# A hybrid attention and mLSTM block: the mLSTM output stored as two float32r parts and reloaded by DMA alone, one head earlier

## The chip, the core and the metric

The kernel runs on one core of a Trainium2 chip. The core has five engines that work side by side, each through a queue of its own, in order: TensorE (PE, matmuls; its weight loads are shown apart as PEld), VectorE (DVE), ScalarE (ACT), GpSimd (POOL) and SyncE (SP), which here does nothing but issue DMA transfers. Sixteen DMA engines move the data. The metric is the time of one execution on the device in microseconds; the median of several runs counts.

## The reference

One decoder layer on 1,024 tokens of width 1,024. A projection feeds two mixers side by side, differential attention (8 heads) and an mLSTM (4 heads of width 256, chunkwise); both outputs are projected, gated and added. A squared-ReLU MLP follows.

```
h = rms_norm(x, norm_mix_g) * (1 + sc_a) + sh_a
aq, ak, av, mq, mk, mv, mo, mi, mf, ga, gm = split(h @ w_in)
...
ya = diff_attention(aq[0], aq[1], ak[0], ak[1], av, lam, bias_by_dist)      # 8 heads, causal softmax
...
hm = mlstm_chunkwise(mq, mk, mv, mi + b_igate, mf + b_fgate)                # 4 heads
hm = rms_norm(hm, mhn_g)
ym = sigmoid(mo) * hm
merged = sigmoid(ga) * (ya @ w_a) + sigmoid(gm) * (ym @ w_m)
x = x + gt_a * (merged @ w_out)
h = rms_norm(x, norm_ffn_g) * (1 + sc_f) + sh_f
x = x + gt_f * (square(relu(h @ w_ff1)) @ w_ff2)
```

The change concerns `ym`, between the mLSTM that makes it and `ym @ w_m` that uses it.

## The kernel before

**Numbers in two parts.** Every float32 operand of a large matmul is used as a high part (rounded to float32r by an ACT copy) and a low part (DVE: source minus high part); `mm3` then issues three matmuls: high by high, high by low, low by high. `split_lo` (line 139) is the DVE half of such a split, wherever it stands.

**Stages.** After the projections come the four mLSTM heads (about 490 to 745 us in the trace), then the eight attention heads (about 745 to 1,214 us), then the products with `w_a`, `w_out` and the MLP.

**mLSTM, `ml_core`.** A head has four groups g of 256 tokens. The string in the code gives the order of its steps: P (load `ex`, the decay factors), K (`keys`: transpose the keys, scale, split; line 987), W (`weights`: scores `st`, times `ex` at line 958, split into `sw` at 960 and 961), S and C (matmuls `num`, `cps`), I, N (normalise), F (`finish`). `finish(g)` multiplies `hs` by the norm and by `hd["o"][g]` (the gate `mo`; line 1052), transposes four blocks into one PSUM bank `tp` (1058), copies them out with the factor `mhg` on ACT (1063) and stores 256 KB into `ym_d` in DRAM (1064). The last group's F is carried over into the next head.

**Attention, `at_core`.** For a head, S (`soft`: logits `lg` at line 1220, bias and running minimum on DVE at 1226, exp on ACT at 1230, combination on DVE at 1239), T (`turn_p`: transposes 1253, ACT `pth` 1256, DVE `ptl` 1257), Y (`sums`: matmuls `pv`, 1273) and F, for eight blocks of 128 queries. The dots in its string are places where `weave` puts steps of a list `filler`, spread evenly. In heads 0 to 6 the filler is the q/k projection of the next head (`at_qk`, matmuls `ps<-w,hT`, 192 of them for a head) and its preparation (`at_prep`: `raw`, `qe`, `kb`; `qe` is completed by a copy DMA `qe<-qe`, line 1196). In head 7 the filler is the reload of `ym` and 24 steps of `ym @ w_m` (`m_unit`, 12 matmuls `ps<-ym,w` in a step, two steps to a part). The rest of the 32 steps runs after head 7. A part also loads a gate `sg` (1316), applies tanh (1317), multiplies on DVE (1320), which frees its PSUM bank, and stores to `mb_d`.

**Reload.** `reload` has eight steps: a 512 KB DMA from `ym_d` into `w_st` (1305), two ACT copies into the high parts of `ym` (1308), two DVE subtractions into the low parts (line 139). `ym` takes over the four 2 MB tiles (`tag="x"`) that held the layer input `hT`: tile 0 of it (tokens 0 to 511) is free when the first half of head 7's q/k projection is done, tile 1 (tokens 512 to 1,023) when all of it is.

**What sets the order.** The order in each queue is fixed when the kernel is built: a scheduler takes the steps in the order in which the code gives them and moves instructions ahead where their operands allow it. Tiles rotate within a tag; `f` has 5 buffers (among them `ex`, `hs`/`it`, `sg`, `pth`, `ptl`), `m` has 4 (`mo`, `yt`), `w_st` has 2, and PSUM has 8 banks: `mm` 2 (parts of `m_unit` among them), `pa` 3, `pb` 3. DMAs that SP issues use eight semaphores in turn, so a DMA also waits until the one eight places ahead of it has landed.

Of the kernel before, what the change touches and what calls it, by code (L numbers as in the profile page):

```python
# [8 lines left out]
F32 = mybir.dt.float32  # L9
F32R = mybir.dt.float32r  # L10
BF16 = mybir.dt.bfloat16
AF = mybir.ActivationFunctionType
ALU = mybir.AluOpType
# [4 lines left out]
P = 128  # L18
S = 1024
D = 1024  # L20
NT = S // P
KT = D // P
AH = 8
# [13 lines left out]
def kernel(  # L37
# [7 lines left out]
    nc = tc.nc  # L45
# [4 lines left out]
    dp = ctx.enter_context(tc.tile_pool(name="dp", bufs=1, space=DRAM))  # L50
    wp = ctx.enter_context(tc.tile_pool(name="wp", bufs=2))
# [7 lines left out]
    def wt(tag, shape, name, dt=F32):  # L59
        return sp.tile(shape, dt, name=name, tag=tag, bufs=BUFS[tag])  # L60

    def bank(tag, name):
        return pp.tile([P, 512], F32, name=name, tag=tag, bufs={"mm": 2, "pa": 3, "pb": 3}[tag])


    ya_d = dp.tile([D, S], F32, name="ya_d")
    ym_d = dp.tile([D, S], F32, name="ym_d")
    sga_d = dp.tile([D, S], F32, name="sga_d")
    sgm_d = dp.tile([D, S], F32, name="sgm_d")
    mb_d = dp.tile([D, S], F32, name="mb_d")  # L70
# [39 lines left out]
    def row(v):  # L110
        return v.rearrange("o (k p) -> (o k) p", p=P)
# [22 lines left out]
    def split_lo(dst, src, hi, pool=None):  # L134

        if pool is None:
            turn[0] += 1
            pool = turn[0] % 2
        return (nc.gpsimd if pool else nc.vector).tensor_tensor(dst, src, hi.bitcast(F32), op=ALU.subtract)  # L139
# [136 lines left out]
    def run(steps):  # L276
        for f in steps:
            f()

    def weave(main, filler):  # L280

        n, done = main.count(None), 0
        for f in main:
            if f is not None:
                f()
            if f is None or not n:
                done += 1
                run(filler[(done - 1) * len(filler) // (n or len(main)):done * len(filler) // (n or len(main))])
# [56 lines left out]
    class Group:  # L345
# [35 lines left out]
        pool = (None, True,)[1:]  # L381
# [369 lines left out]
    def gate_unit(i):  # L751

        dst = (sga_d, sgm_d)[i // 4]
        f = (i % 4) * 256
        get_w = once(next_w)

        def out(ps, t, t0):
            sg = wt("f", [P, 512], "sg")
            nc.scalar.copy(sg, ps)
            nc.sync.dma_start(dst[f + t * P:f + (t + 1) * P, t0:t0 + 512], sg)  # L760

        return sum((
            feat_steps(hT, get_w, t * P, t0, "mm", lambda ps, t=t, t0=t0: out(ps, t, t0))
            for t in range(2) for t0 in (0, 512)
        ), [])
# [4 lines left out]
    class Conv(Group):  # L770
# [7 lines left out]
        pool = (False,)  # L778
# [34 lines left out]
    class Gate(Group):  # L813
# [7 lines left out]
        pool = (False,)  # L821
# [12 lines left out]
    class Tok(Group):  # L834
# [7 lines left out]
        pool = (False,)  # L842
# [82 lines left out]
    def ml_core(h, hd, more):  # L925
# [123 lines left out]
        def finish(g):  # L1049
            hs, ssh = state.pop(("hs", g))  # L1050
            for tt in range(2):
                nc.vector.scalar_tensor_tensor(
                    hs[:, tt, :], hs[:, tt, :], ssh[:, tt:tt + 1], hd["o"][g][:, tt, :], op0=ALU.mult, op1=ALU.mult
                )
            tp = bank("pa", "tp")
            for k in range(2):
                for tt in range(2):
                    nc.tensor.transpose(
                        tp[:, k * 256 + tt * P:k * 256 + (tt + 1) * P], hs[:, tt, k * P:(k + 1) * P], ident
                    )  # L1060
            yo = hs
            for k in range(2):
                nc.scalar.activation(yo[:, k, :], tp[:, k * 256:(k + 1) * 256], AF.Copy, scale=mhg[:, k:k + 1])
            nc.sync.dma_start(
                ym_d[h * 256:(h + 1) * 256, g * 256:(g + 1) * 256].rearrange("(k p) t -> p k t", p=P), yo
            )

        def step(f, g):
            return lambda: f(g)
# [3 lines left out]
        for w in ("P0 K0 P1 K1 W0 W1 P2 C0 S0 N0 W2 S1 I1 C1 F0 K2 I2 P3 N1 C2 S2 F1 W3 X0 X1 N2 I3 S3 X2 N3 F2" if h < MH - 1 else "P0 K0 P1 K1 W0 W1 C0 P2 S0 N0 W2 S1 I1 C1 F0 K2 I2 P3 N1 C2 S2 F1 W3 N2 I3 S3 N3 F2").split():  # L1073
            if w == ".":
                steps.append(None)
            elif w[0] == "X":
                if more:
                    i = int(w[1])
                    steps.append((lambda: more[0](0), lambda: more[1](0), lambda: more[1](1))[i])
            else:  # L1080
                steps.append(step(fs[w[0]], int(w[1])))
        return steps, [step(finish, 3)]


# [28 lines left out]
    def at_qk(h, hd):  # L1113

        get_w = once(next_w)
        hd["raw"] = {}

        def out(ps, hf, jj):
            if jj == 0:
                hd["raw"][hf] = wt("u", [P, 4, 256], "raw")  # L1120
            nc.scalar.copy(hd["raw"][hf][:, jj * 2:jj * 2 + 2, :], ps.rearrange("p (t c) -> p t c", t=2))

        return sum((
            tok_steps(hT, get_w, hf * 4 + jj * 2, "mm", lambda ps, hf=hf, jj=jj: out(ps, hf, jj))
            for hf in range(2) for jj in range(2)
        ), [])
# [170 lines left out]
        return steps, [lambda: finish(1)]  # L1297


    def reload(a, src, pool=None):  # L1300


        def step(t0, k):
            st = wp.tile([P, 2, 512], F32, name="w_st", tag="ws", bufs=2)
            nc.sync.dma_start(st, src[k * P:(k + 2) * P, t0:t0 + 512].rearrange("(k p) t -> p k t", p=P))
            for i in range(2):
                ah, al = a.at(k + i, t0, 512)
                nc.scalar.activation(ah, st[:, i, :], AF.Copy)
                split_lo(al, st[:, i, :], ah, pool)

        return [lambda t0=t0, k=k: step(t0, k) for t0 in (0, 512) for k in range(0, KT, 2)]

    def gated(src, f0, t0):

# [10 lines left out]
    def m_unit(ym, u):  # L1325

        get_w = once(next_w)

        def part(t, t0):
            f0 = u * 256 + t * P  # L1330
            box = []
            steps = feat_steps(
                ym, get_w, t * P, t0, "mm",
                lambda ps: nc.gpsimd.dma_start(mb_d[f0:f0 + P, t0:t0 + 512], box[0](ps)),
            )

            def start():
                box.append(gated(sgm_d, f0, t0))
                steps[0]()

            return [start] + steps[1:]

        return sum((part(t, t0) for t0 in (0, 512) for t in range(2)), [])
# [30 lines left out]
    for j in range(NT + 3):  # L1374
# [10 lines left out]
        if j == 2:  # L1385
# [4 lines left out]
            mhg = par.add(row(mhn_g), 2)  # L1390
# [99 lines left out]
    units = sum((gate_unit(i) for i in range(1)), [])  # L1490
# [10 lines left out]
    for h in range(MH):  # L1501
# [5 lines left out]
        filler = late + gate_unit(h + 1)  # L1507
# [9 lines left out]
    for h in range(AH):  # L1517
        core, nlate = at_core(h, heads[h], vts)
        filler = list(late)
        if h + 1 < AH:  # L1520
            filler += at_qk(h + 1, heads[h + 1])
            if h in AT_GATES:
                filler += gate_unit(AT_GATES[h])
            qs, ps = iter(filler), at_prep(h + 1, heads[h + 1])
            filler = [ps[int(w)] if w in "012345" else next(qs, lambda: None) for w in "qqqqqqqqq012345"] + list(qs)
        else:
            ym = ActX("ym")
            units = sum((m_unit(ym, u) for u in range(4)), [])
            gta = wt("b", [P, D], "gta")
            nc.sync.dma_start(gta, gt_d[0])  # L1530

            nc.vector.tensor_scalar(gta, gta, 0.5, None, op0=ALU.mult)
            wos = {}

            def fetch_wo(r):
                wos[r] = wt("u", [P, D], "wor")
                nc.sync.dma_start(wos[r], w_out[0][r * P:(r + 1) * P, :])

            def gate_wo(r):
                w = wos.pop(r)  # L1540
                nc.vector.tensor_tensor(w, w, gta, op=ALU.mult)
                nc.sync.dma_start(wo_d[r * P:(r + 1) * P, :], w)

            for r in range(8):
                units[12 + 2 * r] = lambda r=r, f=units[12 + 2 * r]: (fetch_wo(r), f())
                units[15 + 2 * r] = lambda r=r, f=units[15 + 2 * r]: (gate_wo(r), f())
            filler += reload(ym, ym_d, False) + units[0:12 * 2]
        weave(core, filler)
        late = nlate
        if h % 2 and h + 1 < AH:  # L1550
            vts = []
            run(at_v(h + 1, vts))
# [279 lines left out]
    class Ff1(Group):  # L1832
# [9 lines left out]
        pool = (False,)  # L1842
# [148 lines left out]
    def b_tile(i, tag, n):  # L1991
        if tag == "x":
            t = xp.tile([P, 2, 4, 512], F32R, name=f"b{n}", tag="x")
            B[i] = lambda k: (t[:, 0, k, :], t[:, 1, k, :])
        else:
            ts = [wt(tag, [P, 2, 512], f"b{n}", F32R) for _ in range(4)]
            B[i] = lambda k: (ts[k][:, 0, :], ts[k][:, 1, :])
# [46 lines left out]
    def left(g, order, load=False):  # L2044
        if load:
            g.load()
        g.weights(order)

    todo = dict(
        a=g0.p1, b=g1.p1, c=g2.load_first, d=g0.p2, e=g3.load_first, f=g1.p2, g=g2.p1, h=g2.p2, i=g3.p1, j=g3.p2,  # L2050
        k=lambda: left(g0, (7, 5), True), l=lambda: left(g1, (7, 5), True), m=g0.p7, n=g1.p7,
        t=lambda: b_tile(5, "x", "t1"),
# [118 lines left out]
    for n in range(7 * NC):  # L2171
# [7 lines left out]
        if n in whole:  # L2179
            q, t0, c0 = whole[n]  # L2180
            nc.sync.dma_start(q, xn_d[t0:t0 + 512, c0:c0 + 512].rearrange("(t p) c -> p t c", p=P))
        if n - 1 in rows:
            q, t0, c0, j = joins[n - 8]
            add(q[:, j], q[:, j], rows.pop(n - 1), False)
        if 7 <= n < 15:
            q, t0, c0, j = joins[n - 7]
# [54 lines left out]
```

## Time and profile before

| | us |
|---|---|
| runs: median (lowest to highest) | 2036.21 (2036.16 to 2036.49) |
| the profiled execution: time of the run, span of the trace | 2033.65, 2031.9 |
| PE busy over the span | 1970.7 (97%) |
| DVE busy | 1636.7 (81%) |
| ACT busy | 1053.0 (52%) |
| mLSTM, 540 to 748 us: PE busy, DVE busy | 200.47 and 132.00 of 208 |
| heads 5 to 7, 1,040 to 1,110 us: PE, DVE | 69.82 and 53.27 of 70 |
| head 7, 1,110 to 1,140 us: PE, DVE | 22.86 and 26.76 of 30 |

The span is that of the trace; the run's own time is 1.75 us longer. An engine's idle time is put down in the trace to whatever event ended it ("releaser"). A line number can be that of a helper: line 139 is every low part, so its rows are told apart by the tile they write (`ym`, `w_lo`). Matmul rows overlap (each is pipelined into the next), so the distance between two starts, not the listed duration, is what a matmul costs in a row of them.

### The profile page before, as it was taken

What the parts mean: (1) busy time and instruction counts of PE and PEld (TensorE: products, weight loads), DVE (VectorE), ACT (ScalarE), POOL (GpSimd) and SP (SyncE); (2) the same over time, 40 slices, a digit from 0 to 9 for tenths busy, and PEclk for the clock granted to TensorE, in tenths of its full rate; (3) what the DMA queues carried; (4) which work ended last, traced back from release to release, by engine and by line L of the source; (5) the groups of instructions that cost most, each with busy time, mean ns of one, the idle gap of its engine ahead of it and who ended that gap; (6) DMA issues with size and microseconds to landing.
All of it is one profiled execution on the core that took longest, in us unless ns stands there. A gap on an engine that the chain in (4) does not pass through costs nothing.

```text
span 2031.9 us, 30206 instructions
## 1 busy us (share of the span) xinstructions
PE 1970.7 (97%) x11193; PEld 1709.9 (84%) x11193; DVE 1636.7 (81%) x2883; ACT 1053.0 (52%) x1983; POOL 55.8 (3%) x150
## 2 busy tenths in 40 slices
PE   5999999999999999999999889999999999999999
PEld 5999998888888899999999668877788888888887
DVE  7977668988766568999978757999867668999896
ACT  5523224544566557777766534546645545433332
POOL 0000000000011000000000100000000000000000
PEclk7999999999999999999999999999999999999999
DMA  8376633335665442322223875603446446755531
GB/s 285 107 221 205 203 113 119 104 104 181 194 169 170 121 116 63 84 63 84 63 83 87 288 263 186 202 22 127 147 145 218 165 151 227 276 181 156 165 114 73
DMA packets 205386, 307.21 MB, mean 151 GB/s; under 512 B 14435, under 2 KB 115454, under 8 KB 205238
## 3 DMA queue, kind: packets, MB, share of 16 engines
q1 hardware_dynamic: 202358, 295.84, 45.9%
q0 software_dynamic: 2880, 9.44, 1.2%
q8 instruction: 88, 1.44, 0.3%
q14 instruction: 60, 0.49, 0.1%
HBM read 212.19 MB, written 84.64 MB: 146 GB/s over the span
## 4 chain that ended last, share of the span: by engine, by line
PE 77%; DVE 8%; DMA 6%; issue 4%; ACT 4%; POOL 1%; SPq 0%; DVEq 0%; POOLq 0%; ACTq 0%
PE cps L329 18%; PE pa L329 10%; PE pc L329 10%; PE pb L329 10%; PE pd L329 5%; PE ps L167 4%; PE ps L166 4%; PE ps L168 4%; PE lg L1220 3%; PE pv L1273 2%; DMA ex<-ea_d 1%; PE ops L586 1%; PE tp L1253 1%; DMA w<-in_w_ff_dram 1%; DMA xt<-in_x_dram 1%
## 5 line engine op out<-in xcount | busy, mean ns | idle before, releaser
L329 PE MATMUL cps<-t_op,s_op 128*128 128x512 f32 x2016 | 466.8, 393 | 2.1 <-DVE t_op L139 1.8
L329 PEld LDWEIGHTS cps<-t_op,s_op 128*128 128x128 f32 x2016 | 377.9, 188 | 88.1 <-DVE t_op L139 2.1
L321 ACT ACTIVATE w_op<-w_st 128x512 fp32r<-128x512 f32 (+1 forms) x197 | 135.9, 705 | 196.2 <-PE pb L329 60.0
L139 DVE TENSOR_TENSOR w_op<-w_st,w_op 128x512 fp32r<-128x512 f32 (+1 forms) x197 | 150.0, 780 | 27.2 <-ACT w_op L321 25.3
L166 PE MATMUL ps<-w_hi,hT 128*128 128x256 f32 x512 | 146.5, 286 | 0.0
L167 PE MATMUL ps<-w_lo,hT 128*128 128x256 f32 x512 | 145.9, 285 | 0.0
L168 PE MATMUL ps<-w_hi,hT 128*128 128x256 f32 x512 | 145.6, 284 | 0.0
L321 ACT ACTIVATE s_op<-act 128x1024 fp32r<-128x1024 f32 x56 | 59.0, 1053 | 149.0 <-PE cps L329 109.5
L1230 ACT ACTIVATE ee<-ee,mneg 128x256 f32<-128x256 f32 (+7 forms) x128 | 98.4, 770 | 12.8 <-DVE mneg L1226 12.5
L1220 PE MATMUL lg<-kb,qe 128*128 128x512 f32 (+3 forms) x384 | 96.0, 357 | 5.2 <-DVE mneg L1226 3.5
L329 PE MATMUL pc<-bt,w_op 128*128 128x512 f32 x384 | 96.7, 399 | 2.4 <-ACT w_op L321 1.4
L167 PEld LDWEIGHTS ps<-w_lo,hT 128*128 128x128 f32 x512 | 97.6, 191 | 1.4 <-issue 0.9
L166 PEld LDWEIGHTS ps<-w_hi,hT 128*128 128x128 f32 x512 | 97.6, 191 | 0.5
L168 PEld LDWEIGHTS ps<-w_hi,hT 128*128 128x128 f32 x512 | 97.6, 191 | 0.3
L329 PE MATMUL pa<-b,w_op 128*128 128x512 f32 x384 | 93.5, 393 | 0.3 <-DVE w_op L139 0.3
L329 PEld LDWEIGHTS pc<-bt,w_op 128*128 128x128 f32 x384 | 71.8, 190 | 22.3 <-DVE w_op L139 5.3
L329 PEld LDWEIGHTS pa<-b,w_op 128*128 128x128 f32 x384 | 72.2, 189 | 15.6 <-DVE w_op L139 0.7
L317 DVE TENSOR_TENSOR acc<-cps,acc 128x512 f32<-128x512 f32 x108 | 71.5, 682 | 11.0 <-PE cps L329 11.0
L1226 DVE CUSTOM_DVE_ANT_0 ee<-lg,bs 128x512 f32<-128x512 f32 (+4 forms) x128 | 69.7, 558 | 8.8 <-PE lg L1220 7.8
L139 DVE TENSOR_TENSOR s_op<-act,s_op 128x1024 fp32r<-128x1024 f32 x56 | 68.2, 1218 | 6.6 <-ACT s_op L321 6.5
L1220 PEld LDWEIGHTS lg<-kb,qe 128*128 128x128 f32 x384 | 60.2, 189 | 14.3 <-DVE mneg L1226 8.5
L329 PE MATMUL pa<-hT,w_op 128*128 128x512 f32 x264 | 64.1, 392 | 0.0
(416 smaller groups left out, 4746.1 us busy)
## 6 DMA issues: line engine op xcount, KB each, us to landing
w_st<-in_w_in_dram SPq DMA_DIRECT2D x72, 512.0 KB, 4.0
act<-act_d SPq DMA_DIRECT2D x56, 512.0 KB, 4.3
w_st<-in_w_ff_dram SPq DMA_DIRECT2D x36, 512.0 KB, 4.1
crow<-in_w_ada_dram SPq DMA_DIRECT2D x32, 512.0 KB, 4.6
w<-in_w_ff_dram SPq DMA_DIRECT2D x32, 512.0 KB, 4.7
act_d<-s SPq DMA_DIRECT2D x40, 256.0 KB, 2.0
act_d<-c SPq DMA_DIRECT2D x33, 256.0 KB, 2.0
act_d<-m SPq DMA_DIRECT2D x33, 256.0 KB, 2.0
```

What stands on the lines that cost most here:

```text
L139: return (nc.gpsimd if pool else nc.vector).tensor_tensor(dst, src, hi.bitcast(F32), op=ALU.subtract)
L166: nc.tensor.matmul(o, lhsT=ah, rhs=bh, start=first, stop=False)
L167: nc.tensor.matmul(o, lhsT=ah, rhs=bl, start=False, stop=False)
L168: nc.tensor.matmul(o, lhsT=al, rhs=bh, start=False, stop=last)
L317: (nc.gpsimd if pick(pool, n) else nc.vector).tensor_tensor(o, a, b, op=ALU.add)
L321: nc.scalar.activation(dst[0], src, AF.Copy)
L329: nc.tensor.matmul(ps, lhsT=p, rhs=q, start=first and k == 0 and r == 0, stop=k == 3 and r == 2, skip_group_check=True,)
L586: nc.tensor.matmul(o, lhsT=a[ra], rhs=w[rb][:, k, :], start=k == 0 and ra == rb and j % 2 == 0, stop=k == KT - 1 and ra == 1, skip_group_c ...
L1220: nc.tensor.matmul(lg[:, 0:max(256, w)], lhsT=hd["q"][hf][e][:, r, q4 * P:(q4 + 1) * P], rhs=hd["k"][e][:, c0:c0 + max(256, w)], start=r = ...
L1226: nc.vector.tensor_tensor_reduce(ee[:, c0:c0 + w], lg[:, 0:w], hd["bs"][:, n - c0 - w:n - c0][:, ::-1], -0.125, first, ALU.add, ALU.min, last,
L1230: nc.scalar.activation(ee[:, 0:n], ee[:, 0:n], AF.Exp, bias=mneg[:, e:e + 1], scale=-1.0, accum_out=ssum[:, e:e + 1])
L1273: nc.tensor.matmul(pv[:, 0:256], lhsT=pts[kk // 4][r][:, (kk % 4) * P:(kk % 4 + 1) * P], rhs=v, start=kk == 0 and r == 0, stop=kk == qi an ...
```

## The change

`finish` writes `ym` as its two parts into two DRAM tensors: ACT makes the high part `yh` in a tile of its own (tag `f`), DVE makes the low part `yl` from the same PSUM bank, in place of the gate tile `mo`, and SP stores both. `reload` becomes four steps of two 1 MB DMAs each, straight into the tiles of `ym`, and moves from the front of head 7's filler to the end of head 6's.

```
-    ym_d = dp.tile([D, S], F32, name="ym_d")
+    ym_d = [dp.tile([D, S], F32, name=f"ym{r}_d") for r in range(2)]
...
-            yo = hs
+            yh, yl = wt("f", [P, 2, 256], "yh", F32R), hd["o"][g].bitcast(F32R)
             for k in range(2):
-                nc.scalar.activation(yo[:, k, :], tp[:, k * 256:(k + 1) * 256], AF.Copy, scale=mhg[:, k:k + 1])
-            nc.sync.dma_start(
-                ym_d[h * 256:(h + 1) * 256, g * 256:(g + 1) * 256].rearrange("(k p) t -> p k t", p=P), yo
-            )
+                v, f = tp[:, k * 256:(k + 1) * 256], mhg[:, k:k + 1]
+                nc.scalar.activation(yh[:, k, :], v, AF.Copy, scale=f)
+                nc.vector.scalar_tensor_tensor(
+                    yl[:, k, :], v, f, yh[:, k, :].bitcast(F32), op0=ALU.mult, op1=ALU.subtract
+                )
+            for d, y in zip(ym_d, (yh, yl)):
+                nc.sync.dma_start(d[h * 256:(h + 1) * 256, g * 256:(g + 1) * 256].rearrange("(k p) t -> p k t", p=P), y.bitcast(F32))
...
-    def reload(a, src, pool=None):
+    def reload(a, src):
...
+        def step(i, k):
+            for r in range(2):
+                nc.sync.dma_start(
+                    a.t[i][r][:, k:k + 4, :].bitcast(F32),
+                    src[r][k * P:(k + 4) * P, i * 512:(i + 1) * 512].rearrange("(k p) t -> p k t", p=P),
+                )
+        return [lambda i=i, k=k: step(i, k) for i in range(2) for k in (0, 4)]
...
+            if h == AH - 2:
+                ym = ActX("ym")
+                filler += reload(ym, ym_d)
         else:
-            ym = ActX("ym")
...
-            filler += reload(ym, ym_d, False) + units[0:12 * 2]
+            filler += units[0:12 * 2]
```

The order in the queues changes at three places. First, DVE at the turn from one mLSTM head to the next. Before:

```order
L262 TENSOR_SCALAR ssh<-ssh 128x2
L1052 SCALAR_TENSOR_TENSOR it<-it,ssh,mo 128x256 x2
L139 TENSOR_TENSOR w_lo<-w_st,w_hi 128x1024
L987 SCALAR_TENSOR_TENSOR kt<-tp,wk,kt 128x256 x4
L958 TENSOR_TENSOR ex<-st,ex 128x512
L139 TENSOR_TENSOR w_lo<-w_st,w_hi 128x1024
L958 TENSOR_TENSOR ex<-st,ex 128x512
L961 TENSOR_TENSOR sw<-ex,sw 128x512 x2
```

In the changed kernel (DVE, the same turn; `mo<-tp,par,yh` is the new low part):

```order
L1052 SCALAR_TENSOR_TENSOR it<-it,ssh,mo 128x256
L1065 SCALAR_TENSOR_TENSOR mo<-tp,par,yh 128x256
L1052 SCALAR_TENSOR_TENSOR it<-it,ssh,mo 128x256
L1065 SCALAR_TENSOR_TENSOR mo<-tp,par,yh 128x256
L139 TENSOR_TENSOR w_lo<-w_st,w_hi 128x1024
L987 SCALAR_TENSOR_TENSOR kt<-tp,wk,kt 128x256 x2
L139 TENSOR_TENSOR w_lo<-w_st,w_hi 128x1024
L987 SCALAR_TENSOR_TENSOR kt<-tp,wk,kt 128x256 x2
L1065 SCALAR_TENSOR_TENSOR mo<-tp,par,yh 128x256
L958 TENSOR_TENSOR ex<-st,ex 128x512 x2
L1065 SCALAR_TENSOR_TENSOR mo<-tp,par,yh 128x256
L961 TENSOR_TENSOR sw<-ex,sw 128x512 x2
```

Four low parts (two groups' F) stand between the rows that feed the next head's first scores, and the second `w_lo` has moved ahead of the two `ex`.

Second, SP's queue around the reload. Before, eight 512 KB loads into `w_st`, the last two of them behind copies of `qe`:

```order
L148 DMA w_st<-in_w_m_dram 128x4x256
L1305 DMA w_st<-ym_d 128x2x512 x6
L1530 DMA gta<-gt_d 128x1024
L1537 DMA wor<-in_w_out_dram 128x1024
L1196 DMA qe<-qe 64x1024 x3
L1305 DMA w_st<-ym_d 128x2x512
L1196 DMA qe<-qe 64x1024
L1537 DMA wor<-in_w_out_dram 128x1024
L1305 DMA w_st<-ym_d 128x2x512
L1682 DMA wa<-in_w_a_dram 128x2x512 x3
```

In the changed kernel (SP; 11869 and 11870 are the high and low tile of tokens 512 to 1,023, and four 1 MB loads of 11867 and 11868, tokens 0 to 511, stand just ahead of these rows):

```order
L1308 DMA ym_11869<-ym_d 128x4x512
L1308 DMA ym_11870<-ym_d 128x4x512
L1308 DMA ym_11869<-ym_d 128x4x512
L1308 DMA ym_11870<-ym_d 128x4x512
L148 DMA w_st<-in_w_m_dram 128x4x256 x2
L1199 DMA qe<-qe 64x1024
L1541 DMA wor<-in_w_out_dram 128x1024
L1199 DMA qe<-qe 64x1024
L1541 DMA wor<-in_w_out_dram 128x1024
L1199 DMA qe<-qe 64x1024
L1534 DMA gta<-gt_d 128x1024
L1199 DMA qe<-qe 64x1024
```

All four copies of head 7's `qe` now stand behind the whole reload and two loads of `w_m`.

Third, PE where head 7 begins (its first `lg` is 128x256). Before, head 6's last `pv` (8 and 8) follow the first two `lg` of head 7, and its last transposes are done:

```order
L166 MATMUL ps<-ym0,w_hi 128x512
L167 MATMUL ps<-ym1,w_hi 128x512
L1220 MATMUL lg<-kb,qe 128x256 x2
L168 MATMUL ps<-ym0,w_lo 128x512
L1183 MATMUL tp<-ksq,raw 128x128 x4
L166 MATMUL ps<-ym0,w_hi 128x512
L1273 MATMUL pv<-va,pth 128x256 x8
L1273 MATMUL pv<-va,ptl 128x256 x8
L1183 MATMUL tp<-ksq,raw 128x128 x4
L1220 MATMUL lg<-kb,qe 128x256 x6
```

In the changed kernel (PE, the same place):

```order
L1186 MATMUL tp<-ksq,raw 128x128 x4
L1223 MATMUL lg<-kb,qe 128x256 x4
L1186 MATMUL tp<-ksq,raw 128x128 x4
L1223 MATMUL lg<-kb,qe 128x256 x2
L1276 MATMUL pv<-va,pth 128x256 x7
L1276 MATMUL pv<-va,ptl 128x256 x7
L1223 MATMUL lg<-kb,qe 128x256 x2
L1223 MATMUL lg<-kb,qe 128x384 x2
L1256 MATMUL tp<-ksq,ee 128x128 x8
L1276 MATMUL pv<-va,pth 128x256 x4
L1223 MATMUL lg<-kb,qe 128x384
L1276 MATMUL pv<-va,pth 128x256 x4
```

The first 48 matmuls of `ym` now stand wholly ahead of head 7 (38 of the 48 did before), while head 6's seventh `pv` group (7 and 7), its eight last transposes and its last `pv` group now stand behind head 7's first logits.

More of the change, by code (lines that the diff above doesn't have):

```diff
@@ L1297, in at_core @@
         return steps, [lambda: finish(1)]
-    def reload(a, src, pool=None):
[L1303 to L1311, printed above, removed]
+    def reload(a, src):
[6 more added lines that the diff above has]
+        return [lambda i=i, k=k: step(i, k) for i in range(2) for k in (0, 4)]
     def gated(src, f0, t0):
```

## The prediction

> **What bounds the kernel now.** I read the page's first and fourth parts for the binding engine, then busy time by stage, since the change touches three: the mLSTM (the new low parts), the end of head 6 (the reload's new place) and head 7 with its tail (the old place).
>
> ```profile
> span 2031.9 us, 30206 instructions
> PE 1970.7 (97%) x11193; PEld 1709.9 (84%) x11193; DVE 1636.7 (81%) x2883; ACT 1053.0 (52%) x1983; POOL 55.8 (3%) x150
> PE 77%; DVE 8%; DMA 6%; issue 4%; ACT 4%; POOL 1%; SPq 0%; DVEq 0%; POOLq 0%; ACTq 0%
> ...
> core 0: us, PE busy (x) PEld busy (x) DVE busy (x) ACT busy (x) POOL busy (x), PEclk, DMA share, GB/s
> 540.00:748.00 208.00, 200.47 (x1296) 179.92 (x1296) 132.00 (x346) 124.54 (x296) 21.52 (x77) 0.99 0.52 149
> 1040.00:1110.00 70.00, 69.82 (x526) 66.29 (x525) 53.27 (x137) 44.25 (x108) 1.08 (x2) 1.00 0.32 95
> 1110.00:1140.00 30.00, 22.86 (x118) 17.29 (x117) 26.76 (x76) 22.43 (x56) 1.08 (x2) 0.94 0.76 246
> 1140.00:1170.00 30.00, 30.00 (x152) 25.36 (x150) 20.05 (x36) 11.55 (x24) 4.33 (x7) 1.00 0.79 278
> 1170.00:1215.00 45.00, 37.03 (x185) 30.40 (x184) 27.76 (x40) 13.37 (x27) 4.19 (x7) 1.00 0.79 271
> ```
>
> PE is the bound nearly everywhere, and the change leaves it every matmul. The time can therefore move only where PE idles. In the mLSTM that is 7.5 us of 208, with DVE busy 63%. From 1,040 to 1,110 it is nothing. At the start of head 7 (1,110 to 1,140) PE idles 7.1 of 30 and DVE is busy 26.76: there DVE binds. In the tail (1,170 to 1,215) PE idles 8.0 of 45 and nothing is full. What PE waited for in these places, by the view of waits (mLSTM, start of head 7, tail; us in total, times, longest), with two waits of DVE in the tail:
>
> ```profile
> PE cps L166 <- DVE ex L958: 3.1, 2, 1.6
> PE num L166 <- ACT sw L960: 2.1, 3, 0.9
> PE num L168 <- DVE sw L961: 1.9, 4, 0.6
> ...
> PE lg L1220 <- DVE mneg L1226: 2.1, 2, 1.7
> PE tp L1253 <- DVE ee L1239: 1.5, 1, 1.5
> PE tp L1253 <- DVE ssum L1235: 1.4, 1, 1.4
> PE lg L1220 <- DMA qe<-qe: 0.9, 1, 0.9
> ...
> PE pv L1273 <- DVE ptl L1257: 3.7, 2, 3.1
> PE tp L1290 <- DVE yt L1284: 2.2, 1, 2.2
> PE ps L166 <- DVE sg L1320: 1.7, 1, 1.7
> ...
> DVE ptl L1257 <- DMA mb_d<-sg: 7.4, 2, 4.7
> DVE sg L1320 <- ACT sg L1317: 6.4, 3, 4.5
> ```
>
> **Term 1, the low parts in the mLSTM: +1.8.** Each of 16 `finish` adds two DVE subtractions of 128x256 out of PSUM. Of the same engine, operation and shape are the rows of line 987 (min, median, max in ns):
>
> ```profile
> L987 DVE SCALAR_TENSOR_TENSOR kt<-tp,wk,kt x24: 466/477/485, 528.4 to 708.8; 128x256 fp32r<-128x256 f32 x24
> ...
> 579.47 0.69 DVE L958 TENSOR_TENSOR ex<-st,ex 128x512 f32<-128x512 f32 x1 [4.35 <-ACT ex L944]
> 580.36 1.23 DVE L139 TENSOR_TENSOR w_lo<-w_st,w_hi 128x1024 fp32r<-128x1024 f32 x1 [0.20 <-ACT w_hi L153]
> 571.76 0.47 SPq L931 DMA_DIRECT2D ex<-ea_d  x1
> ```
>
> 32 x 0.477 = 15.3 us of DVE work; ACT makes the high part with the two copies it made before. DVE has 76 idle us in this stage, so most of it is hidden by matmuls of the next group. It shows where PE already waits on DVE or ACT: the nine waits above (2 + 3 + 4). If a pair stood ahead of each, the loss would be 9 x 2 x 0.477 = 8.6, which is the upper end; the lower end is 0. By the new order, four low parts stand at the turn of a head around `ex`, but DVE idles 4.35 us there for ACT's `ex`, and the next `w_lo` (1.23) has moved ahead of `ex`, out of the way of the `sw` behind it. What is left is the transfer of `ex`, now behind the second store, which waits for the low part: about 1 us later (two low parts), into that 4.35. I take 0.6 at each of two turns and 0.3 at each of two last `sw`: 1.8, nearer the lower end, since of nine waiting places only these have the pair ahead of them.
>
> Where attention begins, the loads of `vr` for head 0 stand behind the last `ym_d` stores, two for each group now: **+0.5**, between 0 (they are ahead of need) and 2.0 (four low parts).
>
> **Term 2, the start of head 7: −1.0.** What leaves it, by the groups of lines there (name, shapes, count; busy us, mean ns; idle before) and DVE's busy time up to the first `sg`:
>
> ```profile
> 1111.00:1136.70 25.70, 22.69 (x65) 0.93 0.77 249
> L139 DVE TENSOR_TENSOR ym<-w_st,ym 128x512 fp32r<-128x512 f32 x7 | 4.7, 677 | 0.0
> L139 DVE TENSOR_TENSOR w_lo<-w_st,w_hi 128x1024 fp32r<-128x1024 f32 x1 | 1.2, 1226 | 0.8 <-ACT w_hi L153 0.8
> L1541 DVE TENSOR_TENSOR wor<-wor,gta 128x1024 f32<-128x1024 f32 x8 | 9.8, 1221 | 5.1 <-DMA wor<-in_w_out_dram 5.1
> ...
> 1104.19 1.28 DVE L1239 SCALAR_TENSOR_TENSOR ee<-ee,ssum 128x1024 f32<-128x1024 f32 x1
> 1106.67 0.69 DVE L1532 TENSOR_SCALAR gta<-gta 128x1024 f32<-128x1024 f32 x1
> 1118.08 1.44 PE L1220 MATMUL lg<-kb,qe 128*128 128x384 f32 x6
> 1113.05 1.11 PE L1273 MATMUL pv<-va,pth 128*128 128x256 f32 x8
> ```
>
> Before, 22.7 busy in 25.7 us up to the first gate product. Seven of the sixteen splits (4.7) and one `w_lo` (1.2) go. In their place come, by the new order, head 6's last combination (1.3), two `ptl` of it (0.7 each), the product of `gta` (0.7), two `wor` (2.4) and two `sg` (0.7 each). The nine other splits (6.1) went beside a full PE before 1,110 and are worth nothing. Adding the new list in the same durations up to the same `sg` gives 18.3, with 2.2 of idle time as before about 20.5, so 5.2 less. But the list is shorter also because head 7 has got less far: 8 `lg`, 18 `pv` and 4 transposes, at most 8 x 0.24 + 18 x 0.14 and some tenths, with the narrow ones about 4.0 of PE, are still to do. 5.2 − 4.0 makes −1.2; I take −1.0. Ends: −7 (all of PE's idle time there) and +4 (all that is left over meets no cover).
>
> PE's wait for `qe` (0.9) I halve, **−0.5**: its four copies move ahead of the last transfers of old, but behind the reload (a rival below).
>
> **Term 3, the tail: −2.0.** The 16 loads and products of `wor` and `w_m` stand earlier, and with 24 filler steps over the same 21 dots, 48 more matmuls of `ym` are done ahead of head 7's first F (156 for 108), so that 132 are left for the stretch of 8.0 us of waits, not 180. Two things act there. The low parts `ptl` and gates `sg` share the five buffers of `f`, and a buffer is free when its store has landed (7.4 us of DVE's waits): with 5.5 parts to store instead of 7.5 the waits of 3.7 and 1.7 shrink, −5.4 at most. Against it, fewer matmuls lie between the last steps of head 7, and its own chain shows (the wait of 2.2 for `yt` may double and `lg` waits may add a little: +3). Between −5 and +3 I take −2.0, since the store's landing is the longer of the two today.
>
> **Term 4, the transfers: 0.**
>
> ```profile
> w_st<-ym_d SPq DMA_DIRECT2D x8, 512.0 KB, 3.7
> qe<-qe SPq DMA_DIRECT2D x32, 256.0 KB, 3.4
> 1093.75 0.29 PE L168 MATMUL ps<-w_hi,hT 128*128 128x256 f32 x1
> 1111.83 0.48 PE L1220 MATMUL lg<-kb,qe 128*128 128x256 f32 x2 [0.90 <-DMA qe<-qe]
> ```
>
> 4.2 MB more are written in a stage with DMA at 0.52, and 8.4 MB are read instead of 4.2, in a stage at 0.32. 278 GB/s at a share of 0.79 means some 352 GB/s when full, so 4.2 MB take 12 us. The first half (tokens 0 to 511) can start at half of head 7's projection, about 1,073 by this trace, and lands at 1,085, ahead of the first matmul of `ym` (1,096). The second starts when the last matmul with `hT` is done (1,093.75) and lands at 1,106; its first matmul stands behind head 7's first four S.
>
> **Sum.** +1.8 + 0.5 − 1.0 − 0.5 − 2.0 = −1.2. The profiled execution took 2,033.65 (span 2,031.9), 2.56 under the median of the runs, 2,036.21; the difference is set against the median: 2,035.0.
>
> [...] The row: `qe`'s copies land a median of 3.4 us after issue, and the one at the start of head 7 was late by 0.9, with at most two 512 KB loads ahead of it. [...] No row of before shows a 1 MB load.
>
> **Rivals.**
>
> *Faster, 2,030.* The reload's 10.7 us of DVE and 9.6 of ACT come off the engine that binds, and what the moved steps bring finds room:
>
> ```profile
> L139 DVE TENSOR_TENSOR ym<-w_st,ym 128x512 fp32r<-128x512 f32 x16 | 10.7, 681 | 3.8 <-ACT ym L1308 3.8
> L1308 ACT ACTIVATE ym<-w_st 128x512 fp32r<-128x512 f32 x16 | 9.6, 626 | 6.6 <-PE ps L167 3.7 <-DMA w_st<-ym_d 2.8
> ```
>
> Then PE's 7.1 of waits at head 7 go with a little of the tail: −8 + 1.8 = −6.2. For it: the waits for `ee` and `ssum` there stand right behind splits. Against it: 9 of 16 splits lay beside a full PE, and the list gets 7 us back in other work.
>
> *Slower, 2,041: `qe` behind the reload.* Head 7's first `lg` needs `qe` at 1,111. Ahead of its copies stand the second half (12 us) and two `w_m` loads (1.0 MB, 3 us), then 3.4 for itself. It decides when the last `hT` matmul comes less than some 17 us before the first S. Before, the distance is 1,110.9 − 1,093.75 = 17.2, so there is no margin; but the new order packs the `hT` matmuls earlier, by about 6 us as I count them. If the queue is full of other work or the rate lower, all of head 7 starts 5 to 6 us late: +6 −1.2.
>
> *Slower, 2,042: the low parts stand on the path* at all nine waits of the mLSTM (+8.6 in place of 1.8), since DVE takes its work in order and PSUM's bank `tp` is held until the low part is read.
>
> **How the numbers follow.** The likeliest case (no change to a few us either way, 2,032 to 2,040 by the ends of its terms) has 0.50, the faster rival 0.28, `qe` 0.13, the low parts on the path 0.09. A measurement of this kernel tells about 0.2% (4.1 us) from no change. The likeliest case gives 0.07 to faster, 0.42 to same and 0.01 to slower; the faster rival 0.25 and 0.03; the slower ones 0.19 and 0.03 to same. Faster 0.32, same 0.48, slower 0.20. The range takes in both signs, from 2,028.5 (the faster rival with a better tail) to 2,041.5.
>
> **What the changed profile would show.** Term 1: the 32 low parts at a mean of 0.48, PE's waits from 540 to 748 within 2 us of 7.1. Term 2: no rows of `ym` on ACT and DVE; PE's waits at head 7's start still 5 to 7 us, on the same `mneg`, `ee`, `ssum`. Term 3: DVE's wait for `mb_d` stores below 5, the wait for `yt` not above 4. Term 4: the second half landed 12 to 15 us after issue, and no wait of `lg` for `qe` over 1 us. I am wrong if `lg` waits for `qe` by several us, if first matmuls of `ym` wait for a transfer, or if head 7's waits vanish.

## The result and the profile after

The changed kernel is slower: 2,052.01 us (median of 6 runs) against 2,036.85, a ratio of 1.0066 (95% interval 1.0051 to 1.008), or 13.4 us. The ratio is worked out from all the runs; the two medians alone would give 1.0074. A second set of runs gave 1.0058 (1.0039 to 1.0077). Two executions far from all others (2,154.6 us of the kernel before, 9,257.3 us of `e7_scores_twice`) are left out of the ratios as slow. The two profiled executions lie further apart than the medians, 2,033.65 and 2,053.11; that of before was quicker than each of the six runs behind its median. So the traces tell where time goes, and the ratios how much.

The page after (its line of engines), and the windows that the prediction showed, of the changed kernel; the last row is one that matters only now, and the fence behind it has its counterpart of before. From 1,040 on the changed kernel is some 9 to 10 us behind by its count of matmuls, so that the same times do not hold quite the same work:

```profile
span 2051.3 us, 30221 instructions
PE 1979.3 (96%) x11193; PEld 1717.5 (84%) x11193; DVE 1640.3 (80%) x2899; ACT 1045.4 (51%) x1967; POOL 56.4 (3%) x150
```

```profile
core 0: us, PE busy (x) PEld busy (x) DVE busy (x) ACT busy (x) POOL busy (x), PEclk, DMA share, GB/s
540.00:748.00 208.00, 195.34 (x1242) 175.90 (x1241) 136.07 (x362) 117.73 (x285) 22.32 (x79) 0.97 0.54 160
1040.00:1110.00 70.00, 69.89 (x539) 67.08 (x538) 44.53 (x116) 36.86 (x90) 1.08 (x2) 1.00 0.54 178
1110.00:1140.00 30.00, 23.71 (x137) 18.35 (x136) 29.08 (x75) 20.88 (x51) 0.02 (x1) 0.97 0.72 222
1140.00:1170.00 30.00, 26.81 (x125) 22.49 (x125) 20.15 (x45) 13.65 (x35) 4.25 (x7) 0.92 0.81 283
1170.00:1215.00 45.00, 41.91 (x208) 35.05 (x207) 26.17 (x47) 14.98 (x29) 2.75 (x5) 0.96 0.58 197
1215.00:1250.00 35.00, 30.93 (x135) 25.37 (x134) 18.48 (x24) 10.82 (x19) 4.33 (x7) 0.90 0.65 214
```

```profile
1215.00:1250.00 35.00, 35.00 (x155) 28.70 (x154) 23.09 (x29) 15.98 (x23) 2.83 (x6) 1.00 0.44 150
```

Two things are to be seen. PE has the same 11,193 matmuls but is busy 8.6 us longer (1,979.3 for 1,970.7), and it idles 10.8 us longer (72.0 for 61.2); together that is the 19.4 us between the spans. The longer busy time goes with the clock: PEclk is 0.90 to 0.96 from 1,140 on, where it was 1.00, and 0.97 for 0.99 in the mLSTM. Idle time grew most in the mLSTM (12.7 us for 7.5). From 1,110 to 1,250 it is 16.6 for 15.1, hardly more in sum, but it lies at other places, and the clock is lower in each row there but the first (0.97 for 0.94).

What PE waited for (first the mLSTM, 540 to 748; then 1,110 to 1,240; last DVE's longest wait there):

```profile
PE cps L166 <- ACT yh L1064: 4.9, 1, 4.9
PE cps L166 <- ACT ex L944: 4.6, 1, 4.6
PE cps L166 <- DVE mo L1065: 1.5, 1, 1.5
...
PE lg L1223 <- DVE mneg L1229: 8.9, 5, 3.2
PE pv L1276 <- ACT pth L1259: 2.3, 1, 2.3
PE tp L1256 <- DVE qe L1195: 2.0, 1, 2.0
...
DVE wor L1545 <- DMA wor<-in_w_out_dram: 12.9, 5, 3.9
```

The waits at the turns of a head, 1.5 and 1.6 before, are 4.6 and 4.9 now. Over the whole mLSTM window the waits listed for PE sum to 12.6 us; 7.1 was the sum before, and the prediction had them within 2 us of it. In head 7 the wait for `mneg` grew from 2.1 (and 0.4 in the tail) to 8.9, and DVE itself stood 12.9 us waiting for loads of `wor` (5.1 over the whole trace of before).

The new steps themselves cost what the rows of before had said, and the loads of 1 MB came in time (low parts: min, median, max ns; loads: size and median us to landing):

```profile
L1065 DVE SCALAR_TENSOR_TENSOR mo<-tp,par,yh x32: 475/479/486, 549.1 to 752.3; 128x256 fp32r<-128x256 f32 x32
ym<-ym_d SPq DMA_DIRECT2D x8, 1024.0 KB, 9.6
```

### The profile page after: what moved, and what is told of

The parts are those of the page before. It is cut to its first block, busy times and chain, and to the rows that moved or that the text cites. A ratio compares the mean times of both kernels' runs of the same rounds, so it can differ in the third digit from the quotient of the medians.

```text
span 2051.3 us, 30221 instructions
## 1 busy us (share of the span) xinstructions
PE 1979.3 (96%) x11193; PEld 1717.5 (84%) x11193; DVE 1640.3 (80%) x2899; ACT 1045.4 (51%) x1967; POOL 56.4 (3%) x150
## 4 chain that ended last, share of the span: by engine, by line
PE 66%; issue 16%; DVE 7%; DMA 6%; ACT 3%; POOL 1%; SPq 0%; POOLq 0%; DVEq 0%; ACTq 0%
PE cps L329 18%; PE pa L329 10%; PE pc L329 10%; PE pb L329 10%; PE pd L329 5%; PE ps L167 2%; PE ps L168 2%; PE ps L166 2%; PE lg L1223 2%; PE pv L1276 1%; DMA ex<-ea_d 1%; DMA w<-in_w_ff_dram 1%; PE ops L586 1%; PE tp L1256 1%; DVE s_op L139 1%
## 5 line engine op out<-in xcount | busy, mean ns | idle before, releaser
L317 DVE TENSOR_TENSOR acc<-cps,acc 128x512 f32<-128x512 f32 x108 | 71.9, 686 | 11.4 <-PE cps L329 11.4
L1223 PEld LDWEIGHTS lg<-kb,qe 128*128 128x128 f32 x384 | 60.9, 191 | 20.6 <-DVE mneg L1229 15.1
```

The source lines that it names most:

```text
L317: (nc.gpsimd if pick(pool, n) else nc.vector).tensor_tensor(o, a, b, op=ALU.add)
L1223: nc.tensor.matmul(lg[:, 0:max(256, w)], lhsT=hd["q"][hf][e][:, r, q4 * P:(q4 + 1) * P], rhs=hd["k"][e][:, c0:c0 + max(256, w)], start=r = ...
```

## The turn of an mLSTM head

The turn from head 0 to head 1, first in the kernel before (DVE, ACT and PE; its `ex` was issued at 571.76), then in the changed kernel (DVE, SP, ACT and PE):

```profile
570.44 0.88 DVE L1052 SCALAR_TENSOR_TENSOR it<-it,ssh,mo 128x256 f32<-128x256 f32 x2 [0.88 <-POOL ssh L263]
573.00 0.85 ACT L1063 ACTIVATE it<-tp,par 128x256 f32<-128x256 f32 x2
577.80 0.28 PE L166 MATMUL cps<-vt,kt 128*128 128x258 f32 x1
580.22 0.39 PE L166 MATMUL cps<-vt,kt 128*128 128x258 f32 x1 [1.54 <-DVE ex L958]
```

```profile
571.91 0.48 DVE L1052 SCALAR_TENSOR_TENSOR it<-it,ssh,mo 128x256 f32<-128x256 f32 x1 [0.88 <-POOL ssh L263]
...
573.32 0.36 SPq L1069 DMA_DIRECT2D ym_d<-yh  x1
573.85 0.36 SPq L1069 DMA_DIRECT2D ym_d<-mo  x1
574.31 0.44 SPq L931 DMA_DIRECT2D ex<-ea_d  x1
...
570.74 0.46 ACT L1064 ACTIVATE yh<-tp,par 128x256 fp32r<-128x256 f32 x1
572.83 0.47 ACT L1064 ACTIVATE yh<-tp,par 128x256 fp32r<-128x256 f32 x1 [1.63 <-DVE mo L1065]
581.37 0.69 ACT L944 ACTIVATE ex<-ex,cold 128x128 f32<-128x128 f32 x2 [4.23 <-POOL ex L941]
582.26 0.45 ACT L1064 ACTIVATE yh<-tp,par 128x256 fp32r<-128x256 f32 x1
...
583.97 0.55 PE L166 MATMUL cps<-vt,kt 128*128 128x258 f32 x1 [4.57 <-ACT ex L944]
```

The second high part waits 1.63 us for the first low part, though it needs nothing of it: both halves write one tile, which the low part reads. The two stores wait for it, and `ex` stands behind them on SP. By the times of the traces `ex` starts 2.55 us later than before, but 1.47 of that had arisen ahead of the turn: the finish itself (DVE, line 1052) begins at 571.91 for 570.44. From there to the load of `ex` it is 2.40 us for 1.32, so the turn delays `ex` by 1.08 us; at the next turn it is 1.88. (With the old finish, in `e2_reload_only`, `ex` is issued at 574.29, as late as here, because that trace runs later as a whole.)

PE has nothing to do until ACT and DVE have used `ex`. In the kernel before, the first six `cps` did not wait for it (577.80); only the second six did (580.22, 1.54). Now all twelve stand behind the wait (583.97). The carried finish's high part stood ahead of `ex` on ACT before (573.00); it now stands behind (582.26), and its low part follows on DVE, so the PSUM bank `tp` that both read comes free later. `cps` takes its banks from the same three (`pa`). That this bank is what the first six `cps` now lack is inferred from the order, not shown.

## Head 7

DVE and PE in the changed kernel, 1,156 to 1,184:

```profile
1158.06 1.23 DVE L1545 TENSOR_TENSOR wor<-wor,gta 128x1024 f32<-128x1024 f32 x1 [2.83 <-DMA wor<-in_w_out_dram]
1162.87 1.22 DVE L1545 TENSOR_TENSOR wor<-wor,gta 128x1024 f32<-128x1024 f32 x1
1164.86 0.69 DVE L1229 CUSTOM_DVE_ANT_0 ee<-lg,bs 128x512 f32<-128x512 f32 x1
1177.52 1.23 DVE L1545 TENSOR_TENSOR wor<-wor,gta 128x1024 f32<-128x1024 f32 x1 [3.88 <-DMA wor<-in_w_out_dram]
...
1165.61 0.80 PE L1223 MATMUL lg<-kb,qe 128*128 128x256 f32 x2 [3.19 <-DVE mneg L1229]
1182.67 1.01 PE L1223 MATMUL lg<-kb,qe 128*128 128x384 f32 x2 [3.09 <-DVE mneg L1229]
```

The products of `wor` are attached to steps 15, 17, ... of the list that fills head 7. With the eight reload steps gone from its front, these come earlier: by the built order the eight stand on DVE behind 12 to 32 of head 7's 48 rows of `mneg`, where they stood behind 30 to 48 before. Their loads have two buffers and are not there yet, so DVE stands still with the softmax queued behind it, and PE waits 3.2 and 3.1 us for `mneg`.

## The clock

PE's busy time and granted clock in stretches of 3.4 us: the first turn and the two waits of head 7 (changed kernel), then a pause of 3.1 us in the tail of before:

```profile
578.50:581.90 3.40, 0.91 (x5) 0.99 1.00 271
581.90:585.30 3.40, 1.33 (x6) 0.50 0.86 215
585.30:588.70 3.40, 3.40 (x18) 0.50 0.94 226
1162.10:1165.50 3.40, 0.32 (x3) 1.00 0.85 258
1165.50:1168.90 3.40, 3.29 (x9) 0.51 0.77 205
1179.20:1182.60 3.40, 0.39 (x2) 1.00 0.90 230
1182.60:1186.00 3.40, 3.33 (x8) 0.50 0.59 233
```

```profile
1168.20:1171.60 3.40, 1.93 (x14) 1.00 1.01 294
1171.60:1175.00 3.40, 1.78 (x9) 1.00 0.47 180
1175.00:1178.40 3.40, 3.02 (x17) 1.00 0.98 257
```

In the changed kernel the three stretches in which PE was busy 0.91, 0.32 and 0.39 us were each followed by one at a clock of 0.50 or 0.51. In the trace of before, the pause of 3.1 us fell into two stretches in which PE was busy 1.93 and 1.78 us, and the clock stayed at 1.00. By the clock's records the trace of before has 17.1 us at half clock behind its first 100 us, that of after 44.4. Over all runs the granted clock differs less: its mean is 0.986 in 106 runs of before and 0.984 in 12 of after, which would be 57 and 66 us at half clock if all the rest was at full clock. By estimate half of the difference, 4 us, is lost if PE is at work all that time. Over the 106 runs of before the time rises by only 0.29 us for each us at half clock, which would make it 2.6. So the clock is an estimated 3 to 4 of the 13.4 us, and more in this pair of traces.

## The experiments

Theories: A, both halves of the change cost time, the mLSTM by what stands in its queues at a turn, head 7 by the order of its steps; B, the reload's new place alone does it; and for the mLSTM, rivals on which of its parts (the low parts, the second store, ACT's order, SP's order). Ratios are to the kernel before, run on the same chip; 0.001 is 2.0 us.

**One half at a time.** `e1_store_only`: the new finish, the old reload of the high part.

```
-            filler += reload(ym, ym_d) ...              # head 6
+            filler += reload(ym, ym_d[0], False) + units[0:12 * 2]   # head 7, as before
```

> The two stores and the low parts in the mLSTM stay; the reload is the old one, in its old place, from the high part alone (so the low part of ym is not used). Theory A (both halves of the change cost: 9 us in the mLSTM, 7 us in head 7): 2045 to 2047, PE at the turns of mLSTM heads waits about 4.6 and 4.9 us as in the changed kernel, two longer stretches at half clock there. Theory B (the whole loss comes from the reload's new place, the mLSTM's waits are made up later): 2036 to 2039.

Measured: 1.0036 (1.0021 to 1.0051), 2,044.3 us; PE waits 4.2 and 4.3 us at the turns. `e2_reload_only`: the old finish, the new reload.

```
-                    src[r][k * P:(k + 4) * P, ...]
+                    src[k * P:(k + 4) * P, ...]          # one tensor, old finish
```

> Old finish with one store; the new reload in head 6, both parts read from the one tensor (its low part is then not the difference). Theory A: 2042 to 2045, with PE's waits of about 3 us for mneg in head 7 behind the products of wor. Theory B: 2049 to 2053. The forecast's own terms for head 7 and the tail: 2032 to 2034.

Measured: 1.0048 (1.0031 to 1.0066), 2,048.1 us. `e1_store_only` is just below what A expected and far above B. `e2_reload_only` by itself decides nothing: its median lies between the two ranges, with PE's wait for `mneg` at 9.1 us (longest 5.3). So B falls: each half costs by itself, 7.3 and 9.8 us. Their sum, 17.1, is above the 13.4 of both together, within the intervals.

**The pace of head 7.** `e4_old_pace` puts eight empty steps where the reload stood; `e5_reload_paced` does so in `e2_reload_only`.

```
-            filler += units[0:12 * 2]
+            filler += [lambda: None] * 8 + units[0:12 * 2]
```

> The changed kernel with eight empty steps where the reload's eight steps stood in head 7, so that the products with ym and the wor steps come at the old pace. If the wor products, moved ahead of their loads on DVE, cause head 7's loss: 2044 to 2047 and DVE's wait for wor loads about 5 us instead of 12.9. If qe behind the reload or the lost cover is the cause: within 2 us of 2052.

> Old finish, new reload, and the old pace of head 7 (eight empty steps): the gain of the reload by transfers alone, without the finish that pays for it; both parts read from one tensor, so the low part is not the difference. If the pace of the wor steps was all of the loss of the reload alone (11.3 us): 2034 to 2038. If the reload costs by itself (qe late behind 4 MB, DMA contention): 2040 to 2046. By the forecast's faster rival: 2029 to 2032.

Measured: 1.0028 (1.0017 to 1.004), 2,041.4 us, and 0.9992 (0.9979 to 1.0004). The first gained more than either rival expected; DVE's wait for loads of `wor` fell from 12.9 to 7.5 us, not to 5. The eight empty steps are worth 7.7 us in the changed kernel and 11.4 us in the reload alone, whose loss they take away entirely. `e14_no_wor_product` leaves the eight products out of the changed kernel, `e15_before_no_product` out of the one before:

```
-                nc.vector.tensor_tensor(w, w, gta, op=ALU.mult)
```

> The changed kernel without the eight products of w_out with gta on DVE (w_out is stored as loaded, so the gate gt_a is left out). If those products, queued on DVE ahead of head 7's softmax and waiting for their loads, make head 7's loss (1.0066 for the changed kernel, 1.0028 at the old pace): 1.002 to 1.004, and PE's waits for mneg of 3 us gone. If the pace of the matmuls with ym makes it: 1.005 to 1.008.

> The kernel before without the same eight products (control: what the products cost by themselves, 9.8 us of DVE). If they are hidden in the kernel before: within 0.2% of it. If they are on its path too: 0.995 to 0.998.

> The changed kernel itself, on the chip of the two runs beside it. 1.0051 to 1.008 of the kernel before, as at first.

Measured: 1.0029 (1.0016 to 1.0042), 1.0 (0.9985 to 1.0014), and 1.0058 (1.0039 to 1.0077) for the changed kernel beside them. The same 9.8 us of DVE work is free in the kernel before and costs 5.9 us in the changed one: it is its place in DVE's queue (5.9 of the 7.7 us that the pace is worth; the rest is within the noise). PE's wait for `mneg` from 1,110 to 1,240 (8.9 in the changed kernel), first with the products gone, then at the old pace:

```profile
PE lg L1223 <- DVE mneg L1229: 2.4, 3, 0.9
```

```profile
PE lg L1223 <- DVE mneg L1229: 2.6, 3, 1.8
```

**The mLSTM, part by part.** All at the old pace (1.0028) except the first, which was run on the changed kernel as it is. `e3_high_first`: both high parts, then both low parts.

```
                 nc.scalar.activation(yh[:, k, :], v, AF.Copy, scale=f)
+            for k in range(2):
+                v, f = tp[:, k * 256:(k + 1) * 256], mhg[:, k:k + 1]
                 nc.vector.scalar_tensor_tensor(
```

> The changed kernel with both ACT copies of a finish ahead of both low parts, so that ACT's second copy does not wait for DVE. If that wait (1.6 us at each turn) is what makes the next head's ex late: 2044 to 2047, PE's waits at the turns back to 1.5 to 2.5. If the order of SP (ex behind two stores) or of ACT (the high part behind ex) decides: within 2 us of 2052.

Measured: 1.0083 (1.0069 to 1.0098). No help: the 1.63 us vanish from ACT, and other waits take their place (`cps` for `ex` 6.4 in four places). `e6_in_place_hf` also writes the high part over `hs`, so that it needs no buffer of its own:

```
-            yh, yl = wt("f", [P, 2, 256], "yh", F32R), hd["o"][g].bitcast(F32R)
+            yh, yl = hs.bitcast(F32R), hd["o"][g].bitcast(F32R)
```

> The changed kernel at the old pace, with the high part written in place of hs (no sixth claimant for the five buffers of f) and both high parts ahead of both low parts. If ACT's order at the turn (the carried high part queued behind the next head's ex because it needs a buffer of f) makes PE's waits of 4 to 5 us: 2035 to 2039, waits at the turns back to 1.5 to 2.5. If the low parts' time on DVE or the ex loads behind two stores decide: 2040 to 2042, as the old pace alone gave (2041.4).

Measured: 1.0032 (1.0019 to 1.0045): ACT's order at the turn is that of before, the first six `cps` again start without a wait (579.77), and nothing is gained: the second six wait 2.9 us for `ex`, and `ips` now waits for the low part (3.6 in two places). `e9_no_low` drops the low parts, `e10_one_store` the second store:

```
-                nc.vector.scalar_tensor_tensor(yl[:, k, :], v, f, ...)      # e9; yh stored twice
-            for d, y in zip(ym_d, (yh, yl)):
+            for d, y in zip(ym_d[:1], (yh,)):                               # e10
```

> The changed kernel at the old pace without the 32 low parts: the high part is stored twice, so the stored low part is the high part. If the low parts' 15.3 us on DVE make the mLSTM's loss (ratio 1.0028 at the old pace, 5.7 us): 2035 to 2038, PE's waits at the turns back to about 1.5. If the second store in SP's queue ahead of ex, or the buffer of f, does: 2040 to 2043.

> The changed kernel at the old pace with the low parts computed but not stored (the reload reads the high part for both). If the low parts on DVE make the loss: 2040 to 2043, as the old pace alone. If the second store does (SP's queue ahead of ex, 4.2 MB more of writes): 2035 to 2038. If each does half: 2038 to 2040.

Measured: 1.0016 (1.0002 to 1.003) and 1.0006 (0.9993 to 1.0019). Taking away the low parts returns 2.4 us, the second store 4.5 us, of the 7.3 between `e4_old_pace` and `e5_reload_paced`. Each of these two differences is good to about 3.6 us: the second is just clear of nothing, the first is not. Without the low parts 4.9 us are still lost against `e5_reload_paced`, so their work on DVE is not the whole cause; how the 7.3 us divide stays open. A late issue of `ex` is not the whole cause either: in the trace of `e10_one_store` it is issued as long after the start of the finish as in the changed kernel (2.38 us for 2.40). But there it lands sooner, a median of 5.8 us after issue, for 6.7 in `e4_old_pace` and 5.9 before. `e8_pool_stores` and `e11_ex_on_pool` move the stores, or the loads of `ex`, from SP to POOL:

```
-                nc.sync.dma_start(d[h * 256:(h + 1) * 256, ...   # e8: nc.gpsimd
-            nc.sync.dma_start(ex, ...                            # e11: nc.gpsimd
```

> The changed kernel at the old pace, with the two stores of a finish issued by POOL instead of SP, so that the loads of ex stand behind no store that waits for a low part. If SP's order makes ex late (about 1 us at each turn, and what the clock adds): 2036 to 2039. If ACT's order or DVE's low parts decide: within 2 us of 2041.4. POOL's own work on ex (the causal masks) could now wait behind the stores: then above 2043.

> The changed kernel at the old pace with the 16 loads of ex issued by POOL, so that they no longer stand in SP's queue behind stores that wait for low parts. If that queue makes ex late: 2035 to 2039 and PE's waits for ex at the turns under 2. If ex waits for a buffer of f, which the stores hold, or if the chain through ACT and DVE decides: 2040 to 2045; POOL's own cost of issuing could make it 2045 to 2048.

Measured: 1.0059 (1.0039 to 1.0079) and 1.0071 (1.0052 to 1.009), worse by 6 and 9 us. POOL's masks on `ex` are then queued behind the transfers: from 540 to 770 POOL stood 30.4 us waiting for `yh` ahead of the stores in the first, and 24.9 us for stores of `yh` to land ahead of the loads in the second. `e12_carry_two` carries the last two finishes into the next head, which puts `ex` ahead of their stores on SP; `e13_before_carry_two` is its control.

```
-  ... X2 N3 F2" if h < MH - 1
+  ... X2 N3" if h < MH - 1                 # F2 is carried with F3
```

> The changed kernel at the old pace, with the last two finishes of an mLSTM head (not the last alone) carried into the next head and both high parts ahead of both low parts. The loads of the next head's ex then stand ahead of these stores on SP. If ex behind the stores makes the loss in the mLSTM: 2034 to 2038, like the reload alone at the old pace. If the low parts and the buffers they hold make it wherever they stand: 2040 to 2045.

> The kernel before, with the same two finishes carried over (control for the run beside it). If the turn is bound by ex: 2033 to 2036, a gain of the carry by itself. If the turn is bound by something else (buffers of f, the scores): within 2 us of before.

Measured: 1.0048 (1.0032 to 1.0064) and 1.0038 (1.0023 to 1.0053). The carry costs 7.7 us by itself, so the pair is inconclusive on SP's order. Counted from the load of `qr`, which stands ahead on the same queue, `ex` was issued no earlier in `e12_carry_two` at the first turn (5.75 us for 5.72 in the changed kernel) and 3.1 earlier at the second. In `e13_before_carry_two` it was 1.8 and 2.0 us earlier than before, and PE's wait of `cps` for `ex` grew all the same (5.3 for 3.1): an earlier `ex` alone is no gain.

**The clock.** `e7_scores_twice` issues the matmuls of the first two scores of heads 1 to 3 twice, where PE waits for `ex`, to see whether work in these waits pays for itself in clock. (The second pass starts its sums afresh, so it writes the same scores; the expectation was mistaken on that.)

```
-                for k in range(2):
+                for k in (0, 1, 0, 1) if h and g < 2 else (0, 1):
```

> The changed kernel at the old pace, with the matmuls of the first two scores of mLSTM heads 1 to 3 issued twice (72 more matmuls, some 8.6 us of PE at 0.119 each; the result of each is doubled, so the output is not the reference's). They run where PE waits 4 to 5 us for the next head's ex. [...] Theory work (PE is the bound, matmuls cost what they take): 2046 to 2050.

Measured: 1.003 (1.0015 to 1.0046). PE busy and clock at the two turns (570 to 590 and 620 to 640), at the old pace and with the scores twice:

```profile
570.00:590.00 20.00, 15.55 (x95) 0.91 0.82 223
620.00:640.00 20.00, 14.61 (x90) 0.91 0.73 224
```

```profile
570.00:590.00 20.00, 17.34 (x112) 0.91 0.86 232
620.00:640.00 20.00, 18.33 (x125) 1.00 0.74 220
```

Some 8.6 us of matmuls cost nothing that can be measured, the second turn has no half clock left, and the clock over all runs is 0.988 for 0.985. That rejects the theory of work (they fill idle time, of which the two long turns have 4 to 5 us each); but a gain from the clock is not seen in the time either, so its price at the turns stays unproven. The median, 2,044.1 us, lies below the 2,046 to 2,050 of the theory of work.

No version that beats the kernel before was found. Of the changed versions two are level with it, `e5_reload_paced` and `e10_one_store`, and both reload a low part that is not the difference.

## Why the prediction was wrong, point by point

- **Term 3, the tail (−2.0): the step that failed.** The prediction saw that the loads and products of `wor` would stand earlier and booked it as a gain. A product that stands earlier than its load can land stops DVE's whole queue (12.9 us of waits for loads of `wor` here): 5.9 us of the loss go when the products are left out (`e14_no_wor_product`). At the changed pace the reload alone costs 9.8 us, at the old pace −1.6. The waits that the term did cost fell: DVE's for stores of `mb_d` from 7.4 to 1.9 us, PE's for `yt` from 2.2 to 0.3. But in `e5_reload_paced` they are as low (1.7 and 0.3) at the old pace, so they did not fall for the term's reason, and the time there is level with before. The prediction weighed filler steps only as cover for PE, not as work that is queued on DVE.
- **Term 2, the start of head 7 (−1.0 and −0.5): not contradicted, not shown.** The run that has it without the change of pace is `e5_reload_paced`, at −1.6 us (−4.3 to +0.8). The 18.3 us of DVE work in it cannot be added up again from the rows shown (22.7 − 5.9 + 7.2 is 24.0); the difference would have to be rows that the shorter list no longer reaches.
- **Term 1, the low parts (+1.8): mis-sized.** The duration was right (0.479 us for 0.477), the turns were rightly named as the place, and the price was 7.3 us (`e4_old_pace` against `e5_reload_paced`; `e1_store_only` gives the same), near the upper end of 8.6. The prediction set the later `ex` (about 1 us, and 1.08 and 1.88 were measured) against DVE's idle 4.35 us at the turn. But that idle time was itself the wait for `ex`, so a later `ex` prolongs it and hides nothing. It also counted only places where PE already waited; the long waits now, 4.6 and 4.9, are those of the first six `cps`, which had waited for nothing. The rest of the 7.3 us is open: the experiments put part of it on the second store, and not clearly any on the low parts' own time on DVE.
- **Attention's entry (+0.5)** was about right in size: the wait of `lg` for `kb` there is 1.3 for 0.3. That the loads of `vr` make it, as forecast, no run shows, so the size may be luck.
- **Term 4, the transfers (0), and the rival of `qe`: right, and rightly unlikely.** The first load was issued at 1,083.2, which is 1,073 in the time of before plus the 10 us lost by then. `lg` did not wait for `qe`'s copies: PE's waits from 1,100 to 1,250 list none, and the four copies landed a median of 4.3 us after issue (5.7 at most). That the transfers ahead of them add up one after another, as the rival has it, no run shows. The eight loads of 1 MB, issued within 16.2 us and several at a time, landed a median of 9.6 us after issue (11.8 at most), and no matmul of `ym` waited for one.
- **The rivals.** That on the low parts came nearest to the mLSTM's price (8.6 for 7.3), with a chance of 0.09, but spread it over nine places where now two turns carry most. None named DVE's queue in head 7. All slower cases together had 0.20.
- **The clock** was in no term. The profile of before showed it, by the row of 20 us in which PE waited 1.56 for `ex` and the clock was 0.91:

```profile
620.00:640.00 20.00, 17.31 (x104) 15.37 (x103) 11.69 (x25) 12.62 (x30) 3.13 (x13) 0.91 0.64 179
```

## What to carry to other kernels

When steps are taken from the front of a list that fills gaps, everything behind them moves forward: ask of each step that moves whether its load will have landed, and what is queued behind it on the same engine. Idle time that is a wait for a transfer does not cover work that delays the transfer (DVE's 4.35 us for `ex` here). And compare kernels of this kind by sets of runs: the kernel before spread from 2,030 to 2,045 us over 106 runs, and one trace of each would have put the loss at 19 us.

## What the runs showed of the hardware

Waits of PE and the clock around them, at the first and second turn of an mLSTM head, before (waits of 1.54 and 1.56 us), then in the changed kernel (4.6 and 4.9 us):

```profile
570.00:590.00 20.00, 17.33 (x115) 15.52 (x114) 12.52 (x27) 12.58 (x32) 3.40 (x13) 1.00 0.67 182
620.00:640.00 20.00, 17.31 (x104) 15.37 (x103) 11.69 (x25) 12.62 (x30) 3.13 (x13) 0.91 0.64 179
```

```profile
570.00:590.00 20.00, 15.11 (x90) 13.67 (x89) 11.22 (x24) 12.32 (x31) 2.89 (x12) 0.83 0.87 223
620.00:640.00 20.00, 15.11 (x87) 13.64 (x86) 11.20 (x29) 11.77 (x30) 2.91 (x12) 0.83 0.85 223
```

The two long waits went with a clock of 0.83 over 20 us. Of the two short ones, equal to 0.02 us, one went with 0.91 and the other with 1.00, and the pause of 3.1 us in the tail of before with 1.00. In these two traces the length of a wait alone did not tell what it cost in clock; that was read from the clock beside it.
